# Matmuls of two PSUM banks interleaved, operand by operand, in the projections and the feed-forward layer of a one-core block

## The chip, the cores and the metric

The kernel runs on one core of one Trainium2 chip. The metric is the device time of one execution in microseconds. Five engines work side by side, each in the order of its own instructions: TensorE (matmuls; in the profile PE, and PEld for the loads of its stationary operand), VectorE (DVE), ScalarE (ACT), GpSimd (POOL) and SyncE (SP), whose queue issues the DMAs here. A matmul multiplies a stationary operand of 128 x 128, loaded by a LDWEIGHTS instruction, with a moving operand of 128 rows and up to 512 columns, and writes or accumulates into a bank of PSUM. There are eight banks of 512 fp32 columns.

## The reference, cut to what matters

One layer of a diffusion transformer on 1024 tokens of 1024 features, in fp32. The two products with large weights that the change touches most are `w_in` and the feed-forward pair:

```
px  = modulate(x, mx[0], mx[1]) @ w_in            # 1024 x 3840
mix = token_mixers(px, ...)                       # scans, short convolution, spatial gate
x1  = layer_norm(ALPHA * x + mx[2] * (mix @ w_out), ...)
h   = modulate(x1, mx[3], mx[4])
a, g = split(h @ ffn_up)                          # 1024 x 5632, two halves of 2816
a   = dwconv3x3(a as a 16 x 64 grid) + conv_b
ffn = (gelu(a) * g) @ ffn_down                    # 2816 -> 1024
out = layer_norm(ALPHA * x1 + mx[5] * ffn, ...)
```

Every fp32 product is computed as three float32r products. Both operands are split into a high part (rounded to float32r) and a low part (the exact rest), and high x high, high x low and low x high are accumulated in the same bank.

## The kernel before

`mm3` (L100 to L104) issues these three matmuls: L102 multiplies the high stationary part with the high moving part, L103 the same stationary part with the low moving part, L104 the low stationary part with the high moving part. All three go to one bank. L102, L103 and L104 therefore stand for nearly all matmuls in the profile.

A *unit* is 128 columns of a weight matrix against all 1024 tokens. It needs two banks, one for each half of the tokens, and 8 feature tiles (kt) x 3 matmuls for each half: 48 matmuls of 512 columns. Before, a unit runs through all 24 matmuls of the first half and then through the 24 of the second:

- `proj` and `proj_fm` compute a unit of `w_in`, in 20 places: three for each of the heads 1 to 3 (`z_head`), one for each head's gate (`gate_head`), five in `short_conv`, two in `spatial_gate`. Each is preceded by `load_unit`, which loads the weights in two DMAs and splits them on ScalarE (L82) and VectorE (L83).
- `banks_up` and `up_half` compute a unit of `ffn_up`. There are 44, taken in the order a(f), g(f), a(f+1), ... for f from 0 to 21. The first three units (0, 22, 1) are issued half by half in an order of their own, `self.first`.
- `ffn_down` works on a token half at a time with all eight banks: four token tiles (t) x two halves of the 1024 output columns (c). It runs over the 22 feature tiles f, and for each over t and c, with one `mm3` of 3 matmuls in each bank; here the stationary operand is a tile of the split activations (`hh`) and the weights move. The last 3 feature tiles of the first token half and the last 7 of the second are kept back as `late` and issued bank by bank at the end.

The banks come from two pools of four, A and B, each used in rotation (`bank`). All of `w_in`'s units use pool A. The scan stages (`scan_levels`, L575 and its neighbours) use B. In `ffn_up` the units of a use A and those of g use B. A bank is free again when its last reader is done. The readers are:

- in a scan head, ScalarE's sigmoids (`scan_z`);
- in `gate_head`, ScalarE (L663) and then VectorE (L664), after which L665 completes the head;
- in `spatial_gate`, VectorE (L824), which first needs the small matmuls of L820 and their evacuation L823;
- in `ffn_up`, for a the two ScalarE reads L953 and L954 of each half, after which VectorE runs the convolution (L964, eight instructions over the whole tile), ScalarE the GELU (L966) and VectorE the product with g (L970), which reads and so frees g's banks.

The order on each engine is made by the framework's planner. It takes instructions by priority (their order in the program, with weights and their splits pulled ahead by `AHEAD` = 350 places) as their inputs and tiles become available in its own timing model. On TensorE it so places scan matmuls between the matmuls of projections.

Of the kernel before, what the change touches and what calls it, by code (L numbers as in the profile page):

```python
# [16 lines left out]
P = 128  # L17
# [14 lines left out]
# columns of the packed per-partition parameters  # L32
# [9 lines left out]
def strided(t, off, dims):  # L42
    """An access pattern over the free bytes of an SBUF tile (offsets in elements)."""
    return bass.AP(t.tensor, t.offset + off, [list(t.ap[0])] + [list(d) for d in dims])


class Builder:
    AHEAD = 350        # how far weights run ahead of the program's order
# [10 lines left out]
    # ---------------------------------------------------------------- tiles  # L59
# [18 lines left out]
    # -------------------------------------------------------------- helpers  # L78
    def split(self, src, hi, lo):
        """hi = src rounded to float32r; lo = the exact rest of it."""  # L80
        nc = self.nc
        nc.scalar.copy(hi, src)  # L82
        nc.vector.tensor_tensor(out=lo, in0=src, in1=hi.bitcast(F32), op=ALU.subtract)  # L83

    def load_unit(self, src, shape, hl=None):
        """Weights from DRAM [128, 1024] into their high and low parts."""
        hi, lo = hl or (self.Wt(shape, nm="wh"), self.Wt(shape, nm="wl"))
        n = shape[0] // 2
        for i in range(2):
            c = slice(i * n, (i + 1) * n)  # L90
            self.load_split(src[:, c], hi[:, c], lo[:, c], (n, shape[1]))
        return hi, lo
# [12 lines left out]

    def rsqrt(self, y, v, n):
        """y = v ** -0.5 for a few columns: first guess from the bits, three Newton steps."""
        nc = self.nc
        t = self.small([n], nm="nwt", bufs=2)
        yi = y.bitcast(I32)  # L110
        nc.vector.tensor_scalar(out=yi, in0=v.bitcast(I32), scalar1=1, scalar2=None, op0=ALU.logical_shift_right)
        nc.vector.tensor_scalar(out=yi, in0=yi, scalar1=-1, scalar2=0x5F3759DF, op0=ALU.mult, op1=ALU.add)
        for _ in range(3):
            nc.vector.tensor_tensor(out=t, in0=v, in1=y, op=ALU.mult)
            nc.vector.scalar_tensor_tensor(out=t, in0=t, scalar=-0.5, in1=y, op0=ALU.mult, op1=ALU.mult)
            nc.vector.scalar_tensor_tensor(out=y, in0=t, scalar=1.5, in1=y, op0=ALU.add, op1=ALU.mult)

    def rsqrt2(self, y, v, n):
        """y = v ** -0.5: square root of ScalarE, reciprocal, one Newton step."""
        nc = self.nc  # L120
        t = self.small([n], nm="nwt1", bufs=4)
        nc.scalar.activation(t, v, AF.Sqrt)
        nc.vector.reciprocal(y, t)
        nc.vector.tensor_tensor(out=t, in0=v, in1=y, op=ALU.mult)
        nc.vector.scalar_tensor_tensor(out=t, in0=t, scalar=-0.5, in1=y, op0=ALU.mult, op1=ALU.mult)
        nc.vector.scalar_tensor_tensor(out=y, in0=t, scalar=1.5, in1=y, op0=ALU.add, op1=ALU.mult)

    def ln_stats(self, tiles, tag, act=False, st=None):
        """Mean and 1/sqrt(var + eps) over the free axis of each tile: [128, n, 2]."""
# [19 lines left out]
    def ln_stats_act(self, x, junk):  # L149
        """The same for one tile, the sums on ScalarE."""  # L150
# [15 lines left out]
    def ada_col(self, j, sc, dst, tiles):  # L166
        """One column of 128 modulations: ada_w[:, 128j:128j+128].T @ silu(c) + ada_b."""
# [14 lines left out]
    def after(self, t, j=5):  # L182
        """Holds a load into t back until the start-up has modulation j."""
        self.nc.vector.tensor_copy(t[:, 0:1], self.mods[:, j:j + 1])
# [11 lines left out]
    # ------------------------------------------------------------- the whole  # L196
    def build(self):
        tc, nc, a = self.tc, self.nc, self.a
        self.NR = 4
        with ExitStack() as ctx:  # L200
# [9 lines left out]
            # the scan's large tiles; later parts of w_out, then of h  # L210
# [30 lines left out]
    def alloc_x2(self, pool, g):  # L241
        """Modulated x_new, feature-major, for token half g: [k2][high, low] of [128, 2, 512]."""
# [15 lines left out]
    def consts2(self):  # L258
        nc = self.nc
        # lower bound: the running sum of a softmax over DEPTH = 1 rows, less its first row  # L260
# [14 lines left out]
        # masks[l][s, t] = 1 where s and t share a block of 2B but not one of B (B = 2**l)  # L275
# [6 lines left out]
        nc.vector.tensor_tensor(out=ii, in0=ii, in1=x, op=ALU.bitwise_xor)      # s xor t  # L282
# [4 lines left out]
    # --------------------------------------------------------------- start-up  # L287
    def startup(self):
        """x to feature-major xm (high, low); z_f, z_b, q of head 0, v of heads 0 and 1 and a part of the short convolution's
        gate as the features arrive, first for the first half of the tokens, then for the second."""  # L290
# [6 lines left out]
        # silu of c and of c_ctx, to come back as rows on every partition  # L297
# [15 lines left out]
        def norm(t, act, n=1):  # L313
            """LN of tiles t to t + n - 1; act: sums on ScalarE."""
# [67 lines left out]
        # products one step behind their features  # L382
# [34 lines left out]
    # ----------------------------------------------------------- token mixers  # L417
    def proj_fm(self, unit, banks):
        """128 columns of w_in for all tokens, features on the partitions."""
        hi, lo = unit  # L420
        for g in range(2):
            s = slice(g * 512, (g + 1) * 512)
            for kt in range(KT):
                self.mm3(banks[g], hi[:, kt, :], lo[:, kt, :], self.xh[kt][:, s], self.xl[kt][:, s], kt == 0, kt == KT - 1)
# [11 lines left out]
    def unit_tm(self, src, w=None):  # L436
        """256 columns, kt in two halves, for the token-major products."""
        return [self.load_unit(src[i], (4, 256), w and (w[:, 2 * i], w[:, 2 * i + 1])) for i in range(2)]

    def proj_tm(self, src, xh, xl, ntt, evac, w=None):  # L440
        """256 columns, tokens on the partitions; two token tiles in a bank."""
# [13 lines left out]
    def step(self, n):  # L455
        """The next pieces of the work that goes between other stages."""
        while n and self.aside:
            self.aside.pop(0)()
            n -= 1
# [60 lines left out]
    def scan_z(self, s, g, zf, zb, zq):  # L520
        """Sigmoids of z_f, z_b (and of their negatives) and silu(q) for token half g."""
# [9 lines left out]
    def scan_prep(self, s, h, z=None):  # L531
# [11 lines left out]
        # the factor 1 - lb of k goes with q, channel by channel  # L543
# [6 lines left out]
    def scan_levels(self, s):  # L550
        """Scores within chunks of 128: blocks of B against their neighbours, B doubling.

        kq holds (without 1 - lb, which q has) k_f * (decay from after s to its block's end), k_b * (decay from its
        block's start to before s), q * (decay from its block's start to t), q * (decay
        from t to its block's end); F[d] at B*j holds the decay over block j."""
# [9 lines left out]
        for l in range(7):  # L565
# [14 lines left out]
            # to blocks of 2B  # L580
# [12 lines left out]
    def scan_states(self, s, h, vt):  # L593
# [4 lines left out]
        for d in range(2):  # L598
# [3 lines left out]
            # the last chunk of a scan leaves no state  # L602
# [38 lines left out]
        # times 1 / sqrt(mean over the head's 128 values + eps), token by token  # L641
# [14 lines left out]
    def gate_head(self, O, h):  # L656
        """O * hg_norm_g * silu(g)"""
# [9 lines left out]
    def ctx_mods(self):  # L667
        """The context's normalised tiles and its modulations, in pieces."""
# [24 lines left out]
    def ctx_prep(self):  # L693
        """The context, modulated, feature-major, in high and low parts."""
# [14 lines left out]
    def ctx_states(self, ch, cl):  # L709
        """The states that the context leaves to both scans (without the factor 1 - lb)."""  # L710
# [6 lines left out]
        for h in range(H):  # L717
            fk = self.S((2, 2, TC), nm="cfk")     # [f_f, f_b], [k_f, k_b]
# [10 lines left out]
            for d in range(2):  # L729
# [4 lines left out]
                # decay from after s to the end (forward), from the start to before s (backward)  # L734
# [46 lines left out]
    def spatial_gate(self):  # L781
        nc, a = self.nc, self.a
        rows = self.S((2, 512), nm="sgrow")     # ln_g, ln_b
        nc.sync.dma_start(rows[:, 0, 0:256], a["sg_ln_g"].broadcast_to([P, 256]))
        nc.sync.dma_start(rows[:, 1, 0:256], a["sg_ln_b"].broadcast_to([P, 256]))
        wsb = self.S((6, P), nm="sgwb")         # w[g].T, then b_s over the two heads of each pair
# [41 lines left out]
    # -------------------------------------------------------- output projection  # L828
    def gate_row(self, m, row):
        """Modulation m as a row on every partition."""  # L830
# [13 lines left out]
    def ln_rows(self, y, lng, lnb):  # L844
        """y = LN(y) * lng + lnb, in place."""
# [5 lines left out]
    def wout_load(self, which, op=None):  # L851
        """w_out's rows with the gate (modulation 2) on their columns, in two parts."""
# [66 lines left out]
    def modulate2(self, pool, ys, t0):  # L919
        """LN and modulation 3, 4 of x_new's tiles from t0 on, feature-major into x2."""  # L920
# [18 lines left out]
    # ------------------------------------------------------------------- FFN  # L939
# [32 lines left out]
    def banks_up(self, f):  # L972
        """Columns f of ffn_up; the first few in an order that waits last for the second half of the tokens."""
# [10 lines left out]
        return [self.up_half(u, g, "A" if f < FT else "B") for g in range(2)]  # L984
# [8 lines left out]
    def ffn_down(self, dn):  # L993
        nc, a = self.nc, self.a
        rows = None
        for g in range(2):
# [8 lines left out]
            for f in range(FT):  # L1005
# [24 lines left out]
                if f < FT - LAST:  # L1030
                    for t in range(4):
                        for c in range(2):
                            work(t, c, f, hh, wh, wl)
# [39 lines left out]
    def finish(self, y, t, lng, lnb, st):  # L1073
        """out = LN(y) * lng + lnb"""
# [10 lines left out]
def layout(x):  # L1085
    """The inputs laid out for the kernel; values untouched."""
    import numpy as np
    c = np.ascontiguousarray
    w = x["w_in"][0]                                      # [1024, 3840]
    fm = w.reshape(KT, P, 30, P).transpose(2, 1, 0, 3)    # [30, 128 p, 8 kt, 128]  # L1090
    tm = lambda m: c(m.reshape(2, 4, P, -1, 256).transpose(3, 0, 2, 1, 4))   # [n, 2, 128 p, 4 kt, 256]
# [32 lines left out]
```

## Time and profile before

| | |
|---|---|
| runs of the kernel before | 1353.97 and 1355.95 us, median 1354.96 us |
| span of the profiled execution | 1354.2 us, 17543 instructions |
| stage of the mixers (projections, scans, gates) | to about 526 us |
| output projection and second modulation | about 526 to 634 us |
| ffn_up | about 634 to 1105.7 us |
| ffn_down | 1105.7 to about 1345 us, the final normalisation after it |
| DMA | 135.14 MB, 100 GB/s on average |

The page of the profile gives first the busy time of each engine, its share of the span and its instructions, then a strip of 40 slices in tenths, then the chain of work that ended last, and then groups of instructions by line. In such a group, `psA<-x,wh` is a matmul into a bank of pool A with a moving operand x and a stationary operand wh; `x352` is the count. The time that is printed for a matmul includes a modelled end that overlaps the next one, so the distance between the starts of two matmuls, or the length of a stretch over the count, is the pace.

### The profile page before, as it was taken

How to read it: one execution, taken by the hardware profiler on the slowest of the kernel's cores; microseconds unless marked ns; L12 is line 12 of the kernel's file. 1: busy time of each engine (PE TensorE's matmuls, PEld its weight loads, DVE VectorE, ACT ScalarE, POOL GpSimd, SP SyncE). 2: the span in 40 equal slices, each digit the busy share in tenths (PEclk: the TensorE clock that was granted, in tenths of full speed). 3: DMA queues.
4: the chain of work that ended last, by engine and by line, in shares of the span. 5: the costliest groups of instructions: out<-in, count | busy, mean ns of one | idle time of the engine just before them, and what ended most of it. 6: DMA issues, size and time to landing. Idle time of an engine off the chain costs nothing.

```text
span 1354.2 us, 17543 instructions
## 1 busy us (share of the span) xinstructions
PE 1319.4 (97%) x6730; PEld 1114.1 (82%) x6730; DVE 945.0 (70%) x1735; ACT 472.1 (35%) x878; POOL 1.7 (0%) x8
## 2 busy tenths in 40 slices
PE   4999999999999999999999999999999999999997
PEld 3888988898888887877888888888888888888885
DVE  7979954869688688886876757575656664349357
ACT  4744544433331424434322222222222233223330
POOL 0000000000000000000000000000000000000000
PEclk9999999999999999999999999999999999999998
DMA  9672410132131444221222111211111033235332
GB/s 331 249 242 77 133 63 31 32 116 81 40 112 60 137 148 156 99 104 62 95 77 78 63 63 47 68 50 54 47 47 47 31 115 135 93 109 201 111 105 82
DMA packets 60900, 135.14 MB, mean 100 GB/s; under 512 B 7168, under 2 KB 7824, under 8 KB 60816
## 3 DMA queue, kind: packets, MB, share of 16 engines
q1 hardware_dynamic: 60816, 134.02, 29.2%
q8 instruction: 53, 0.87, 0.3%
q14 instruction: 31, 0.25, 0.1%
HBM read 125.59 MB, written 8.40 MB: 99 GB/s over the span
## 4 chain that ended last, share of the span: by engine, by line
PE 82%; DVE 9%; DMA 4%; ACT 3%; issue 1%; DVEq 0%; SPq 0%; ACTq 0%
PE psA L102 16%; PE psA L103 16%; PE psA L104 16%; PE psB L103 9%; PE psB L102 9%; PE psB L104 9%; PE psB L575 4%; PE psB L614 1%; DMA r<-in_w_out 1%; DMA cada<-in_ada 1%; DVE adat L172 1%; ACT O L639 1%; DMA adat<-in_ada 1%; DVE bnst L137 1%; DVE wl L83 1%
## 5 line engine op out<-in xcount | busy, mean ns | idle before, releaser
L83 DVE TENSOR_TENSOR wl<-r,wh 128x512 fp32r<-128x512 f32 x160 | 104.3, 687 | 155.8 <-ACT wh L82 149.9
L82 ACT CAST wh<-r 128x512 fp32r<-128x512 f32 x160 | 92.5, 619 | 311.5 <-PE psB L103 160.7
L102 PE MATMUL psA<-x,wh 128*128 128x512 f32 x352 | 137.3, 390 | 0.8 <-ACT x L82 0.8
L104 PE MATMUL psA<-x,wl 128*128 128x512 f32 x352 | 137.2, 390 | 0.0
L103 PE MATMUL psA<-x,wh 128*128 128x512 f32 x352 | 137.2, 390 | 0.0
L102 PE MATMUL psB<-x,wh 128*128 128x512 f32 x352 | 137.0, 389 | 0.0
L104 PE MATMUL psB<-x,wl 128*128 128x512 f32 x352 | 136.9, 389 | 0.0
L103 PE MATMUL psB<-x,wh 128*128 128x512 f32 x352 | 136.9, 389 | 0.0
L102 PE MATMUL psA<-xh,wh 128*128 128x512 f32 x320 | 126.7, 396 | 0.0
L103 PE MATMUL psA<-xl,wh 128*128 128x512 f32 x320 | 126.4, 395 | 0.0
L104 PE MATMUL psA<-xh,wl 128*128 128x512 f32 x320 | 125.8, 393 | 0.0
L964 DVE SCALAR_TENSOR_TENSOR h<-a,par,h 128x945 f32<-128x945 f32 (+2 forms) x96 | 117.4, 1223 | 7.1 <-ACT a L954 4.2
L964 DVE SCALAR_TENSOR_TENSOR hk<-a,par,hk 128x945 f32<-128x945 f32 (+2 forms) x80 | 97.6, 1223 | 5.6 <-ACT a L954 3.4
L102 PEld LDWEIGHTS psA<-x,wh 128*128 128x128 f32 x352 | 66.0, 188 | 14.7 <-ACT x L82 1.2
L102 PEld LDWEIGHTS psB<-x,wh 128*128 128x128 f32 x352 | 66.1, 188 | 13.9 <-DVE x L83 0.3
L103 PEld LDWEIGHTS psB<-x,wh 128*128 128x128 f32 x352 | 66.1, 188 | 13.8
L103 PEld LDWEIGHTS psA<-x,wh 128*128 128x128 f32 x352 | 66.1, 188 | 13.6
L104 PEld LDWEIGHTS psB<-x,wl 128*128 128x128 f32 x352 | 66.1, 188 | 13.6
L104 PEld LDWEIGHTS psA<-x,wl 128*128 128x128 f32 x352 | 66.1, 188 | 13.6
L104 PEld LDWEIGHTS psA<-xh,wl 128*128 128x128 f32 x320 | 60.2, 188 | 11.8
L103 PEld LDWEIGHTS psA<-xl,wh 128*128 128x128 f32 x320 | 60.2, 188 | 11.8 <-issue 0.2
L102 PEld LDWEIGHTS psA<-xh,wh 128*128 128x128 f32 x320 | 60.2, 188 | 11.7 <-issue 0.2
(316 smaller groups left out, 2787.7 us busy)
## 6 DMA issues: line engine op xcount, KB each, us to landing
r<-in_wup SPq DMA_DIRECT2D x88, 256.0 KB, 2.7
r<-in_w_down SPq DMA_DIRECT2D x88, 256.0 KB, 2.9
r<-in_win SPq DMA_DIRECT2D x56, 256.0 KB, 2.8
ada<-in_ada SPq DMA_DIRECT2D x24, 512.0 KB, 3.8
adat<-in_ada SPq DMA_DIRECT2D x16, 512.0 KB, 6.7
r<-in_ada SPq DMA_DIRECT2D x26, 256.0 KB, 3.0
cada<-in_ada SPq DMA_DIRECT2D x11, 512.0 KB, 5.4
x<-in_x SPq DMA_DIRECT2D x8, 512.0 KB, 5.8
```

Of the source, the lines that this page charges most:

```text
L82: nc.scalar.copy(hi, src)
L83: nc.vector.tensor_tensor(out=lo, in0=src, in1=hi.bitcast(F32), op=ALU.subtract)
L102: mm(out, lh, rh, start=first, stop=False)
L103: mm(out, lh, rl, start=False, stop=False)
L104: mm(out, ll, rh, start=False, stop=last)
L137: nc.vector.bn_stats(out=st[:, c, :], in_=x[:, c * 512:(c + 1) * 512])
L172: nc.vector.tensor_tensor_reduce(out=t, in0=t, in1=sc[:, i * n:(i + 1) * n], scale=1.0, scalar=0.0 if i == 0 else acc[:, 0:1], op0=ALU.mul ...
L575: nc.tensor.matmul(b[:, c, :], A[:, t0:t0 + P], strided(kq, 3 * T + t0, [[2 * B, P // (2 * B)], [B - T, 2], [1, B]]), start=c == 0, stop=c ...
L614: nc.tensor.matmul(b[:, c, :], KTt[:, g * 4 + c, :], vt[:, g * 4 + c, hv], start=c == use[g][0], stop=c == use[g][-1])
L639: nc.scalar.activation(O[:, k, :], b[:, c, :], AF.Square, accum_out=ss[:, k:k + 1])
L964: nc.vector.scalar_tensor_tensor(out=o, in0=a3[:, r0 + di:r1 + di, c0 + dj:c1 + dj], scalar=cw(i, j), in1=o, op0=ALU.mult, op1=ALU.add)
```

## The change

A new helper `mm3_pair` takes two banks, one pair of stationary parts and two pairs of moving parts. It issues the six matmuls operand by operand, and each operand for both banks before the next. `proj_fm`, `banks_up` (all but the first three units) and the main part of `ffn_down` use it. In the units the loop over kt is now outermost, and both banks are allocated ahead of it. The `late` steps of `ffn_down`, `up_half` for the first three units, the token-major products (`proj_tm`), the start-up and the output projection keep `mm3`. Apart from this the diff removes comments and docstrings only.

```
+    def mm3_pair(self, outs, lh, ll, rhs, first, last):
+        mm = self.nc.tensor.matmul
+        for i, (l, r) in enumerate(((lh, 0), (lh, 1), (ll, 0))):
+            for o, m in zip(outs, rhs):
+                mm(o, l, m[r], start=first and i == 0, stop=last and i == 2)
...
     def proj_fm(self, unit, banks):
         hi, lo = unit
-        for g in range(2):
-            s = slice(g * 512, (g + 1) * 512)
-            for kt in range(KT):
-                self.mm3(banks[g], hi[:, kt, :], lo[:, kt, :], self.xh[kt][:, s], self.xl[kt][:, s], kt == 0, kt == KT - 1)
+        for kt in range(KT):
+            self.mm3_pair(banks, hi[:, kt, :], lo[:, kt, :],
+                          [(self.xh[kt][:, g * 512:(g + 1) * 512], self.xl[kt][:, g * 512:(g + 1) * 512]) for g in range(2)],
+                          kt == 0, kt == KT - 1)
...
         u = self.load_unit(self.a["wup"][f], (KT, P))
-        return [self.up_half(u, g, "A" if f < FT else "B") for g in range(2)]
+        banks = [self.bank("A" if f < FT else "B") for _ in range(2)]
+        for kt in range(KT):
+            x = [[self.x2[kt // 2][p][g][:, kt % 2, :] for p in range(2)] for g in range(2)]
+            self.mm3_pair(banks, u[0][:, kt, :], u[1][:, kt, :], x, kt == 0, kt == KT - 1)
+        return banks
...
                 if f < FT - LAST:
                     for t in range(4):
-                        for c in range(2):
-                            work(t, c, f, hh, wh, wl)
+                        s = slice(t * P, (t + 1) * P)
+                        self.mm3_pair(banks[t], hh[0][:, s], hh[1][:, s],
+                                      [(wh[:, c * 512:(c + 1) * 512], wl[:, c * 512:(c + 1) * 512]) for c in range(2)],
+                                      f == 0, f == FT - 1)
```

## The prediction

> **What bounds the kernel now.** I read the page's first two parts, then the chain, to see which engine is the limit and whether that holds in every stage.
>
> ```profile
> PE 1319.4 (97%) x6730; PEld 1114.1 (82%) x6730; DVE 945.0 (70%) x1735; ACT 472.1 (35%) x878; POOL 1.7 (0%) x8
> ...
> PE   4999999999999999999999999999999999999997
> ...
> PEclk9999999999999999999999999999999999999998
> ...
> PE 82%; DVE 9%; DMA 4%; ACT 3%; issue 1%; DVEq 0%; SPq 0%; ACTq 0%
> ```
>
> TensorE is full in every slice but the first and the last, at the full granted clock, and carries 82% of the chain. The time is therefore the number of matmuls times their pace, plus the moments in which TensorE waits. Those are few:
>
> ```profile
> PE psB L411 <- DVE x L163: 17.5, 3, 11.4
> PE psA L102 <- ACT xh L414: 1.3, 1, 1.3
> PE psA L103 <- DVE wl L83: 1.3, 1, 1.3
> PE psB L652 <- DVE OT L647: 1.1, 4, 0.3
> ...
> PE psA L103 <- DVE wo L83: 0.8, 1, 0.8
> PE psA L102 <- ACT x L82: 0.8, 1, 0.8
> ...
> PE psB L820 <- DVE vs L810: 0.4, 2, 0.2
> ```
>
> That is the view of waits for TensorE (total, times, longest). The 17.5 us are the start-up. All other waits sum to 7.8 us, so removing stalls can give little. What is left is the pace. The printed duration of a matmul overlaps its neighbours, so I take the pace from the table of stretches, as length over count:
>
> ```profile
> 470.20:488.20 18.00, 18.00 (x152) 18.00 (x151) 14.01 (x23) 7.63 (x13) 0.00 (x0) 1.00 0.43 134
> 700.00:1080.00 380.00, 380.00 (x1678) 314.53 (x1678) 242.69 (x265) 100.80 (x159) 0.00 (x0) 1.00 0.17 55
> 1115.00:1205.00 90.00, 90.00 (x398) 74.51 (x397) 34.64 (x55) 31.27 (x57) 0.00 (x0) 1.00 0.34 115
> ```
>
> The columns are length, then PE, PEld, DVE, ACT and POOL busy with counts, the granted clock, DMA. About two matmuls of a count only reach in over an edge. The first row is a stage of 256-column matmuls: 18.00 / 150 = 120.0 ns. The second is ffn_up, 512 columns, 24 in a row into one bank: 380 / 1676 = 226.7 ns. The third is ffn_down, where the bank changes every third matmul: 90 / 396 = 227.3 ns, or 226.7 with one more in the count. From 120.0 and 226.7, 256 columns stream in 106.7 ns and a fixed 13.3 ns comes with every matmul whatever its length. Those 13.3 ns are all that a better order could remove.
>
> **The change part by part.** First, how many matmuls it touches:
>
> ```profile
> L102 PE MATMUL psA<-x,wh 128*128 128x512 f32 x352 | 137.3, 390 | 0.8 <-ACT x L82 0.8
> L102 PE MATMUL psA<-xh,wh 128*128 128x512 f32 x320 | 126.7, 396 | 0.0
> L103 PEld LDWEIGHTS psB<-x,wh 128*128 128x128 f32 x352 | 66.1, 188 | 13.8
> L103 PEld LDWEIGHTS psA<-x,wh 128*128 128x128 f32 x352 | 66.1, 188 | 13.6
> ```
>
> Of ffn_up's 44 units 41 go the new way (the first three keep up_half): 41 x 48 = 1968. The projections' 320 per line are 320 x 3 = 960, that is 20 projections. ffn_down has 19 + 15 feature steps before its late ones, 24 matmuls each: 816. Together 3744 of 6730. None is added or removed, and no DMA, evacuation or load moves in the program.
>
> *Shared stationary operand.* Before, the second of each three (L103) has the same stationary operand as the first: 2 of 6 neighbours share. After, it is 4 of 6. The rows above say what sharing does now: L103 still has its own LDWEIGHTS, 352 for 352 matmuls, and the page counts 6730 loads for 6730 matmuls. The timeline around a change of bank shows its pace:
>
> ```profile
> 1094.16 0.39 PE L102 MATMUL psA<-x,wh 128*128 128x512 f32 x1
> 1094.39 0.39 PE L103 MATMUL psA<-x,wh 128*128 128x512 f32 x1
> 1094.62 0.39 PE L104 MATMUL psA<-x,wl 128*128 128x512 f32 x1
> 1094.84 0.39 PE L102 MATMUL psB<-x,wh 128*128 128x512 f32 x1
> 1095.07 0.39 PE L103 MATMUL psB<-x,wh 128*128 128x512 f32 x1
> ```
>
> L103 starts 0.23 us after L102 (same stationary operand), L104 0.23 after L103 (another one). Sharing is worth nothing here: cost 0.
>
> *No bank twice in a row.* L104 to L102 above goes to another bank and starts 0.22 us later, as within a bank, and the ffn_down stretch has the same 226.7 to 227.3 ns. Cost 0. What the trace never shows is both at once, another bank and the same stationary operand. I bound it by the nearest rows: at best the fixed 13.3 ns goes, at worst the pace is off by the 0.6 ns between the two stretches, 3744 x 0.6 = 2.2 us either way. I take 0, since each half alone shows 0; the best end is a rival below.
>
> [...]
>
> *Both banks finish together.* Before, a unit's first bank was complete 24 matmuls (5.4 us) ahead of its second, and was evacuated under it. Now both end with the unit, and both must be free at its start. In ffn_up the pools A and B alternate and a pair of banks comes back only three units (3 x 48 x 0.2267 = 32.6 us) after its end, so 5 us are covered. In the projections, all in pool A, a pair comes back after one unit, 10.9 us. The latest evacuation there is the first gated head's: its unit's last matmul starts at 385.69 us, its second bank is read at 393.59, and the unit that wants the bank starts at 400.72.
>
> ```profile
> 385.69 0.39 PE L104 MATMUL psA<-xh,wl 128*128 128x512 f32 x1
> ...
> 393.59 0.68 DVE L664 TENSOR_TENSOR G<-psA,G 128x512 f32<-128x512 f32 x1
> ...
> 400.72 0.39 PE L102 MATMUL psA<-xh,wh 128*128 128x512 f32 x1
> ```
>
> A second such read of 0.68 us ends at 394.95: 5.8 us to spare, cost 0. Two places are tighter.
>
> The last gated head takes the bank that the spatial gate reads last:
>
> ```profile
> 512.49 2.84 PE L820 MATMUL psB<-sgwb,vs 128*64 128x128 f32 x48 [0.22 <-DVE vs L810]
> 515.26 0.50 PE L103 MATMUL psA<-xl,wh 128*128 128x512 f32 x1
> 515.45 0.69 DVE L824 TENSOR_TENSOR sgo<-sgo,psA 128x512 f32<-128x512 f32 x1
> ...
> 534.73 0.50 PE L103 MATMUL psA<-wo,mh 128*128 128x512 f32 x1 [0.84 <-DVE wo L83]
> ```
>
> Its projection goes on at 515.26; a pair needs the second bank at once, and L824 frees it at 515.45 + 0.69 = 516.14. That is a new wait of up to 0.9 us. But TensorE waits 0.84 us at 534.73 anyway, for a part of w_out that arrives no later than now: the one wait goes into the other. I take 0; the ends are 0 and 0.9.
>
> At the turn from ffn_up to ffn_down the last convolution is late next:
>
> ```profile
> 1095.86 0.77 ACT L953 ACTIVATE h<-psA,par 128x512 f32<-128x512 f32 x1
> 1096.54 0.57 ACT L954 COPY a<-psA 128x512 f32<-128x512 f32 x1
> ...
> 1097.14 10.03 DVE L964 SCALAR_TENSOR_TENSOR h<-a,par,h 128x945 f32<-128x945 f32 x8 [0.38 <-ACT a L954]
> ...
> 1108.37 1.29 DVE L970 TENSOR_TENSOR h<-h,psB 128x512 f32<-128x512 f32 x2
> ...
> 1109.80 0.39 PE L102 MATMUL psB<-dwh,dhr 128*128 128x512 f32 x1
> 1110.03 0.39 PE L103 MATMUL psB<-dwl,dhr 128*128 128x512 f32 x1
> ```
>
> From ScalarE's first read of the second half (1095.86) to the convolution (1097.14) are 1.28 us. With both halves left to the end it is twice that, and L970, which frees the last two banks of pool B, ends at 1109.66 + 1.28 = 1110.94. ffn_down's fourth token tile takes these banks; as a pair its second matmul would start at 1110.03 and now waits to 1110.94: +0.9 us, with nothing behind it to absorb it. The ends are 0 (the planner puts other matmuls first) and 1.3.
>
> *The planner's order.* In the mixers it slots scan matmuls between projection matmuls. A new order can shift which of the small waits occur: by the wait rows at most all 7.8 us vanish or as much again appears. I take 0.
>
> **The sum.** The profiled execution spans 1354.2 us; 1354.2 + 0 + 0 + 0.9 = 1355.1. The runs' median, 1354.96, is 0.8 above that span, so 1355.9 us.
>
> **The rivals.**
> 1. *Faster: the fixed 13.3 ns goes where neighbours share the operand and change bank.* 3744 x 4/6 = 2496 matmuls x 13.3 ns = 33.2 us: 1355.9 - 33.2 = 1322.7. For it: only this combination is unseen, and two hidden causes of equal size would each alone show nothing. Against it: L103 pays in full for a repeated operand, a changed bank pays in full, and the load is issued every time. It decides at 27.1 / 2496 = 10.9 ns. Chance 5%.
> 2. *Slower: units wait for their pair of banks.* All 61 units (20 + 41) now ask for two free banks at their first matmul. A wait of 27.1 / 61 = 0.44 us at each is 2%; at 1 us each the time is 1355.9 + 61 = 1417. Against it: ffn_up has some 28 us to spare, the projections 5.8 us at the tightest ordinary place. Chance 3%.
> 3. *Slower: the clock drops.* At half clock the 213.4 ns of streaming double; 127 matmuls of it make 27.1 us, and the whole 3744 would give 1355.9 + 799 = 2155. The ffn_down stretch, which goes through eight banks in turn, has a granted clock of 1.00. Chance 1%. [...]
> 4. *The change does not do what it says*, because the planner breaks up the pairs: the time stays at 1355, inside my own case.
>
> **How the numbers follow.** My own case has 91%: 1355.9, with the pace's 2.2 us and about 7 us of shifted waits to either side, 1347 to 1365. Outside 2% (1327.9 to 1382.1, about what a measurement of this kernel can tell from no change) lie only rivals 1 to 3: faster 5%, slower 3 + 1 = 4%, the same 91%. The range 1347 to 1365 leaves out these 9% and some 8% for smaller gains or losses of pace.
>
> **What would show it.** The stretch inside ffn_up should again give 226 to 228 ns per matmul with as many loads as matmuls; 215 there would prove rival 1. The granted clock stays 1.00. A TensorE wait of about 0.9 us for L970 should appear at the start of ffn_down, and the wait at 534.73 should shrink if one appears at 515. Conversely a TensorE wait on ScalarE or VectorE readers of pool A or B at many units would prove rival 2. I am wrong above all if repeated operand and changed bank together differ from either alone.

## The result and the profile after

| | before | after |
|---|---|---|
| median of the runs | 1354.96 us | 1367.74 us (1367.71 and 1367.77) |
| span of the profiled execution | 1354.2 us | 1365.9 us |
| mean granted clock of TensorE | 0.997 | 0.995 |

The ratio is 1.0092, with a 95% interval of 1.0062 to 1.0121: 12.8 us slower, within 2%, and above the predicted range of 1347 to 1365. In the changed kernel all matmuls of pairs stand on L111, and the lines of before that lie behind the new helper are 7 higher (L663 is L670, L664 is L671, L665 is L672, L970 is L977).

The page of the changed kernel: busy time and the strip of 40 slices for TensorE.

```profile
PE 1322.1 (97%) x6730; PEld 1113.8 (82%) x6730; DVE 941.7 (69%) x1735; ACT 469.4 (34%) x878; POOL 1.7 (0%) x8
...
PE   4999999999999997999999999999999999999997
```

The work is the same, with a load for each matmul as before. The strip has one new digit: a 7 in slice 16, 512 to 546 us, where the output projection begins. The stretch inside ffn_up, in the view of stretches (length, then PE, PEld, DVE, ACT and POOL busy, the granted clock, DMA):

```profile
700.00:1080.00 380.00, 380.00 (x1678) 314.53 (x1677) 243.41 (x271) 98.52 (x157) 0.00 (x0) 1.00 0.18 57
```

1678 matmuls in 380 us again: the pace has not moved. What moved are waits. The view of waits of TensorE (total, times, longest):

```profile
PE psA L104 <- DVE ml L83: 3.7, 1, 3.7
PE psA L102 <- ACT mh L82: 3.2, 1, 3.2
PE psA L111 <- ACT wh L82: 1.5, 1, 1.5
PE psA L103 <- DVE xl L422: 1.3, 1, 1.3
...
PE psB L111 <- DVE h L977: 1.1, 1, 1.1
```

The first two and the last are new. mh and ml are the split parts of the mixers' output, one token tile at a time: the operand with which `out_proj` begins. The timeline of TensorE there (start, length, then the instruction, and in brackets the idle time before it and its releaser):

```profile
528.87 0.61 PE L111 MATMUL psA<-xh,wl 128*128 128x512 f32 x2
532.69 0.50 PE L102 MATMUL psA<-wok,mh 128*128 128x512 f32 x1 [3.21 <-ACT mh L82]
...
533.49 0.40 PE L103 MATMUL psA<-wok,mh 128*128 128x512 f32 x1
537.54 0.80 PE L104 MATMUL psA<-wok,ml 128*128 128x512 f32 x1 [3.66 <-DVE ml L83]
538.13 0.63 PE L102 MATMUL psA<-wok,mh 128*128 128x512 f32 x1
538.56 0.63 PE L103 MATMUL psA<-wok,mh 128*128 128x512 f32 x1
...
541.00 0.39 PE L103 MATMUL psA<-wok,mh 128*128 128x512 f32 x1
```

At 528.87 the last two matmuls of the last gated head's unit start. In the 8.7 us from there to 537.54 TensorE starts only four more, and the ones behind the second wait start 0.43 us apart instead of 0.23. From 537.54 to 541.00 are 8 steps: 3.46 us where 8 x 0.23 = 1.84 are usual, 1.6 more; the granted clock there is 0.55 on average. The two waits and the slow steps make 3.2 + 3.7 + 1.6 = 8.5 us; the 0.84 us at 534.73 that before had is gone, so 7.7 net. With the 1.1 us on h that is 8.8 of the 11.7 by which the spans differ. (The row names h because L977, which frees the bank as it reads g out of it, writes h.)

Why is mh late? ScalarE's timeline, first before, then after:

```profile
520.80 0.60 ACT L663 ACTIVATE G<-psA 128x512 f32<-128x512 f32 x1 [25.35 <-PE psA L104]
521.30 0.49 ACT L82 CAST mh<-O 128x128 fp32r<-128x128 f32 x2
```

```profile
529.29 0.60 ACT L670 ACTIVATE G<-psA 128x512 f32<-128x512 f32 x1 [31.15 <-PE psA L111]
529.79 2.16 ACT L82 CAST wo<-r 128x512 fp32r<-128x512 f32 x4
531.86 0.60 ACT L670 ACTIVATE G<-psA 128x512 f32<-128x512 f32 x1
532.35 0.49 ACT L82 CAST mh<-O 128x128 fp32r<-128x128 f32 x2
```

In both kernels ScalarE stands idle for 25 to 31 us in front of its first read of the last head's banks, and the splits mh come behind that read. Before, the first bank was complete in the middle of the unit, so the read, and with it the splits, ran under the second half. Now the first bank is complete only when the unit ends. VectorE repeats the pattern for ml:

```profile
529.92 0.69 DVE L671 TENSOR_TENSOR G<-psA,G 128x512 f32<-128x512 f32 x1 [5.35 <-ACT G L670]
530.53 2.49 DVE L83 TENSOR_TENSOR wo<-r,wo 128x512 fp32r<-128x512 f32 x4
532.93 0.68 DVE L671 TENSOR_TENSOR G<-psA,G 128x512 f32<-128x512 f32 x1
...
534.68 1.28 DVE L672 SCALAR_TENSOR_TENSOR O<-O,par,G 128x1024 f32<-128x1024 f32 x1
535.88 1.29 DVE L881 TENSOR_TENSOR r<-r,gate 128x512 f32<-128x512 f32 x2
...
537.20 0.28 DVE L83 TENSOR_TENSOR ml<-O,mh 128x128 fp32r<-128x128 f32 x1
```

ml is at the end of a row of 7.3 us of VectorE work that began when the unit ended, and none of that work is ml's own input. (Its inputs are mh, split at 532.35, and the output O of an earlier head; L672 writes the O of the last head.)

### The profile page after: what moved, and what is told of

Read it like the earlier page. It is cut to its first block, busy times and chain, and to the rows that moved or that the text cites. A ratio compares the mean times of both kernels' runs of the same rounds, so it can differ in the third digit from the quotient of the medians.

```text
span 1365.9 us, 17541 instructions
## 1 busy us (share of the span) xinstructions
PE 1322.1 (97%) x6730; PEld 1113.8 (82%) x6730; DVE 941.7 (69%) x1735; ACT 469.4 (34%) x878; POOL 1.7 (0%) x8
## 4 chain that ended last, share of the span: by engine, by line
PE 81%; DVE 10%; ACT 4%; DMA 3%; issue 2%; DVEq 0%; SPq 0%; ACTq 0%
PE psA L111 35%; PE psB L111 23%; PE psA L104 4%; PE psA L102 4%; PE psA L103 4%; PE psB L582 4%; DMA cada<-in_ada 1%; PE psB L621 1%; DVE adat L179 1%; PE psB L102 1%; PE psB L104 1%; PE psB L103 1%; ACT O L646 1%; DVE h L971 1%; DVE wl L83 1%
## 5 line engine op out<-in xcount | busy, mean ns | idle before, releaser
L83 DVE TENSOR_TENSOR wl<-r,wh 128x512 fp32r<-128x512 f32 x160 | 104.0, 687 | 126.2 <-ACT wh L82 126.2
L111 PE MATMUL psB<-x,wh 128*128 128x512 f32 x672 | 179.6, 389 | 0.0
L111 PE MATMUL psA<-x,wh 128*128 128x512 f32 x640 | 171.1, 389 | 0.0
L111 PEld LDWEIGHTS psB<-x,wh 128*128 128x128 f32 x672 | 126.1, 188 | 26.2
L111 PEld LDWEIGHTS psA<-x,wh 128*128 128x128 f32 x640 | 120.0, 188 | 25.1
L111 PE MATMUL psB<-x,wl 128*128 128x512 f32 x336 | 103.4, 389 | 0.0
L111 PE MATMUL psA<-xh,wh 128*128 128x512 f32 x320 | 101.1, 394 | 1.6 <-ACT wh L82 1.5
L111 PE MATMUL psA<-xh,wl 128*128 128x512 f32 x320 | 102.2, 396 | 0.0
L111 PE MATMUL psA<-xl,wh 128*128 128x512 f32 x320 | 101.5, 394 | 0.0
L111 PE MATMUL psA<-x,wl 128*128 128x512 f32 x320 | 98.4, 389 | 0.0
L111 PE MATMUL psB<-dwh,dh 128*128 128x512 f32 x264 | 76.1, 389 | 0.0
L111 PE MATMUL psA<-dwh,dh 128*128 128x512 f32 x264 | 76.0, 389 | 0.0
L111 PEld LDWEIGHTS psB<-x,wl 128*128 128x128 f32 x336 | 63.1, 188 | 13.1
L111 PEld LDWEIGHTS psA<-xh,wh 128*128 128x128 f32 x320 | 59.2, 188 | 13.9 <-ACT wh L82 1.9
L111 PEld LDWEIGHTS psA<-x,wl 128*128 128x128 f32 x320 | 60.1, 188 | 12.5
L111 PEld LDWEIGHTS psA<-xl,wh 128*128 128x128 f32 x320 | 59.7, 188 | 12.2 <-issue 0.2
L111 PEld LDWEIGHTS psA<-xh,wl 128*128 128x128 f32 x320 | 59.2, 188 | 11.5 <-issue 0.2
L582 PE MATMUL psB<-kq,A 128*128 128x128 f32 x448 | 60.1, 288 | 0.9 <-ACT A L576 0.7
L582 PEld LDWEIGHTS psB<-kq,A 128*128 128x128 f32 x448 | 55.7, 192 | 6.1 <-ACT A L576 5.7
```

The lines of the kernel that those rows point to most:

```text
L111: mm(o, l, m[r], start=first and i == 0, stop=last and i == 2)
L582: nc.tensor.matmul(b[:, c, :], A[:, t0:t0 + P], strided(kq, 3 * T + t0, [[2 * B, P // (2 * B)], [B - T, 2], [1, B]]), start=c == 0, stop=c ...
```

## The experiments

Three theories. *Theory 1*: in-order queues. The splits of the output projection's first token tile stand behind the last head's reads on ScalarE and VectorE, and a pair lets those reads begin only at the unit's end; one unit of 61 carries nearly all of the loss. *Theory 2*: the loss is spread over the mixers, where both banks of each unit end together. *Theory 3*: the pairs themselves run slower. One expectation below names a fourth as rival 4 (not that of the prediction): both banks come free too late for the next writer. Kernels were timed against the kernel before on the same chip. Its medians there were 1355.32 us (for gate3_by_bank, before_late_bank_first, ffn_pairs_only and proj_pairs_only), 1354.48 us (for before_gate3_pair, split0_before_reads, gate3_down0_by_bank and after_fill) and 1355.43 us (for split0_last_a_by_bank and before_split0_first). Its single executions lay between 1352.55 and 1359.16 us.

### One unit bank after bank

**gate3_by_bank**: the changed kernel, only the last gated head's unit as before.

```
-        z = self.proj(16 + h)
+        z = self.proj(16 + h, pair=h < H - 1)    # pair=False: the loop of before in proj_fm
```

> The changed kernel, but the unit of the last gated head (one of 61 pair units) runs bank after bank as before. Theory 1, queue: the time is lost where the output projection starts, because its operands' splits stand in ScalarE's and VectorE's queues behind the last head's reads, and with a pair both reads come only when the unit ends; TensorE's two waits there are 3.2 and 3.7 us against 0.8 before. Then 5 to 7 us come back: 1361 to 1363 us, and both waits go. Theory 2, spread: pairs upset the order of the whole mixer stage and the last head only shows the sum: 1366 to 1368 us, the waits move elsewhere. Theory 3, pace of pairs: 1367 us.

Measured: 1357.7 us, ratio 1.0016 [1.0006, 1.0025]. Both waits are gone from its list of waits, whose longest behind the start-up is now 1.5 us, and with them the slow steps; h stays:

```profile
PE psB L111 <- DVE h L982: 1.2, 1, 1.2
```

This speaks for theory 1 and against 2 and 3. It gave back about 10 us where 5 to 7 were expected, which the slow steps below explain in part.

### The converse: one unit as a pair

**before_gate3_pair**: the kernel before, with `mm3_pair` in that unit alone (`z = self.proj(16 + h, pair=h == H - 1)`).

> The kernel before with one part of the change alone: only the unit of the last gated head has its two banks interleaved. Theory 1: nearly all of the loss, 8 to 10 us, so 1363 to 1366, with the waits on mh and ml there. Theory 2: one unit of 61, 1355 to 1356.

Measured: 1364.16 us, ratio 1.0072 [1.0058, 1.0085]. Its two longest waits behind the start-up are the same as in the changed kernel:

```profile
PE psA L104 <- DVE ml L83: 3.7, 1, 3.7
PE psA L102 <- ACT mh L82: 3.2, 1, 3.2
```

So 48 of the 3744 matmuls that changed order cost 0.7% of the time.

### No pair at all, the late bank read first

**before_late_bank_first**: the kernel before, all banks filled as there; only the order of the last head's two reads is turned in the program.

```
-        for g in range(2):
+        for g in range(2) if h < H - 1 else (1, 0):
```

> The kernel before, without any pair; only the last gated head evacuates its two banks in the order second, first in the program. The planner then puts the splits of the output projection behind both of the head's reads on ScalarE, as in the changed kernel. Theory 1, queue: TensorE waits for mh and ml at the start of the output projection, though every unit still runs bank after bank: 3 to 6 us above before, 1358 to 1361 us. Theories 2 and 3: within 1 us of before, 1354 to 1356 us.

Measured: 1360.7 us, ratio 1.004 [1.0026, 1.0054]. Both waits appear though every unit runs bank after bank:

```profile
PE psA L104 <- DVE ml L83: 2.9, 1, 2.9
...
PE psA L102 <- ACT mh L82: 0.9, 1, 0.9
```

ScalarE's timeline shows what the edit did:

```profile
524.42 0.60 ACT L663 ACTIVATE G<-psA 128x512 f32<-128x512 f32 x1 [25.21 <-PE psA L104]
...
529.86 0.60 ACT L663 ACTIVATE G<-psA 128x512 f32<-128x512 f32 x1 [2.48 <-PE psA L104]
530.35 0.49 ACT L82 CAST mh<-O 128x128 fp32r<-128x128 f32 x2
```

The bank that is complete first is still read first, in the middle of the unit. But the splits mh now stand behind the second read, which comes only when the unit ends (its last matmul starts at 529.43). That fits theory 1 alone. (The profiled execution, 1364.1 us of span, lies above the median; its list also has a wait of 2.6 us on wl at 469 us, in the mixers, which is not part of this effect.)

### The halves of the change

**ffn_pairs_only** keeps the pairs of `ffn_up` and `ffn_down` and computes all projections bank after bank; **proj_pairs_only** is the reverse.

```
-    def proj_fm(self, unit, banks):
+    def proj_fm(self, unit, banks, pair=False):          # ffn_pairs_only
...
+        return [self.up_half(u, g, "A" if f < FT else "B") for g in range(2)]   # proj_pairs_only, and work(t, c, ...) in ffn_down
```

> Pairs in ffn_up and ffn_down only (2784 of the 3744 matmuls); all projections bank after bank. Theories 1 and 2: only the wait for L977 at the start of ffn_down is left, 1.3 us: 1356 to 1357 us. Theory 3, pace: 2784/3744 of the 12.8 us, 9.5 us: 1364 us.

> Pairs in the 20 projections only (960 of the 3744 matmuls); ffn_up and ffn_down as before. Theories 1 and 2: all but the 1.3 us of ffn_down: 1366 to 1367 us. Theory 3, pace: 960/3744 of the 12.8 us, 3.3 us: 1358 us.

Measured: 1357.08 us, ratio 1.0012 [1.0003, 1.0021], and 1365.01 us, ratio 1.007 [1.0058, 1.0082]. The projections alone came out 1 us under what was expected; their wait on ml is 2.8 us instead of 3.7. The 2784 paired matmuls of the feed-forward layer cost at most 0.2%. The list of waits of ffn_pairs_only has the one on h, and one on xl in the start-up, where nothing is paired:

```profile
PE psA L103 <- DVE xl L422: 1.2, 1, 1.2
PE psB L111 <- DVE h L982: 1.1, 1, 1.1
```

Theory 3 falls.

### The suspected queue, with every pair kept

**split0_before_reads**: the changed kernel with all its pairs; the first token tile's seven splits that do not need the last head are issued between that head's matmuls and its reads. The eighth stays where it was.

```
         z = self.proj(16 + h)
+        if h == H - 1:
+            self.early_split()       # split() of mix[kt][:, 0:P] for kt in self.order[:-1]
         G = self.S(nm="G")
...
-        split(0)
+        mh, ml = mhl[0] = self.early
+        self.split(self.mix[order[-1]][:, 0:P], mh[:, order[-1], :], ml[:, order[-1], :])
```

> All pairs stay as in the changed kernel, the unit of the last gated head included. Only the order of work on ScalarE and VectorE differs: the first token tile's seven splits that do not need the last head stand ahead of the last head's reads. Theory 1 (the splits wait behind reads that come late): the two waits on mh and ml, 3.2 and 3.7 us, go, and so does the slow stretch behind them, so the time falls by 7 to 9 us to 1359 to 1361. Theory 2 (the loss is in the unit itself or spread over the mixers): 1366 to 1368. Rival 4 (both banks are free too late for the next writer): the waits stay, 1366 to 1368.

Measured: 1356.99 us, ratio 1.0017 [1.0008, 1.0026], better than expected. ScalarE's timeline, with L672 for the read, and TensorE's:

```profile
519.48 0.30 ACT L82 CAST mh<-sgo 128x128 fp32r<-128x128 f32 x1 [1.29 <-DVE sgo L838]
527.62 0.60 ACT L672 ACTIVATE G<-psA 128x512 f32<-128x512 f32 x1 [7.84 <-PE psA L111]
```

```profile
527.20 0.62 PE L111 MATMUL psA<-xh,wl 128*128 128x512 f32 x2
527.66 0.40 PE L102 MATMUL psA<-wok,mh 128*128 128x512 f32 x1
...
528.13 0.39 PE L104 MATMUL psA<-wok,ml 128*128 128x512 f32 x1
```

The last of the seven splits starts as soon as its input, the spatial gate's sgo, is there, and is done 8 us ahead of the first read. So in the changed kernel it was their place in the queue, and no input, that held the splits back. (Why the planner had put them behind the reads is not shown.) TensorE goes from the unit into the output projection without a gap. Theory 1 is shown by adding the suspected cost where no pair is, and by taking it away where all pairs are.

### The rest of the loss

The wait on h at the start of `ffn_down` is what is left. **gate3_down0_by_bank**: gate3_by_bank, and the first step of `ffn_down` bank after bank too (`if g == 0 and f == 0: work(t, c, ...)`).

> The changed kernel with the unit of the last gated head bank after bank, as in gate3_by_bank, and the first step of ffn_down too (f = 0, g = 0). Theory 1: the wait on h of 1.2 us goes as well, and what is left of the pairs costs nothing: 1355 to 1357, 1 to 1.5 below gate3_by_bank. If the remaining 2 us were the price of the pairs themselves: no change, 1357 to 1358.

Measured: 1359.11 us, ratio 1.0034 [1.0023, 1.0046]: a miss. The order in which `ffn_down` asks for its banks does not matter, for the wait is as long as it was:

```profile
PE psB L102 <- DVE h L982: 1.1, 1, 1.1
```

Why it is 1.4 us above gate3_by_bank stays open; its wait on xl of 1.6 us at 92 us, in the start-up, was 0.2 in gate3_by_bank, and neither edit touches that stage.

The cause of the wait lies in the unit before the last, the last convolved one. ScalarE's timeline of the changed kernel behind that unit, then VectorE's:

```profile
1105.81 0.77 ACT L960 ACTIVATE h<-psA,par 128x512 f32<-128x512 f32 x1
...
1106.95 0.79 ACT L960 ACTIVATE h<-psA,par 128x512 f32<-128x512 f32 x1
```

```profile
1108.25 8.79 DVE L971 SCALAR_TENSOR_TENSOR h<-a,par,h 128x945 f32<-128x945 f32 x7 [1.53 <-ACT a L961]
1116.95 1.29 DVE L83 TENSOR_TENSOR dwl<-r,dwh 128x512 fp32r<-128x512 f32 x2
1118.16 1.20 DVE L971 SCALAR_TENSOR_TENSOR h<-a,par,h 128x945 f32<-128x945 f32 x1
1120.54 0.69 DVE L977 TENSOR_TENSOR h<-h,psB 128x512 f32<-128x512 f32 x1 [1.18 <-ACT h L973]
```

L960 and the copy L961 of each half, shown by the two L960, all come behind the unit. So the convolution begins 3.2 us after the unit ends (at 1105.01, when the next one starts) instead of 2.3 (1094.84 to 1097.14 before), 0.9 us later. A second delay comes on top: two weight splits (L83) now stand ahead of the eighth convolution instruction, where before they stood behind all eight, and GELU and the product wait 1.2 us more. Together the first product ends some 2 us later, at 1121.23, and the matmul that waits for it, at 1121.28, is the first one of a pair. So the order within the pair does not matter. **split0_last_a_by_bank**: split0_before_reads, and that one unit bank after bank.

```
+        if f == FT - 1:
+            return [self.up_half(u, g, "A") for g in range(2)]
```

> split0_before_reads, and beside it the last convolved unit of ffn_up (f = FT - 1) bank after bank. By the trace the wait on h at the start of ffn_down comes from a unit earlier than it looks: with a pair both banks of that unit end together, ScalarE reads the first of them (0.67 and 0.50 us) only then, and the convolution and all behind it start some 1.2 us later. If so, the wait of 1.1 us on h is gone and the time is 1 to 1.5 us under split0_before_reads (1356.99 there, so 1355.5 to 1356), the time of before. If the wait comes from the following unit (the gate's), it stays and the time does not change.

Measured: 1355.61 us, ratio 1.0004 [0.9995, 1.0013]. The reads (L968 there) are apart again, the first half's under the second half. The eight convolution instructions follow one another without the two splits between them, and no wait on h is left in its list of waits:

```profile
1090.70 0.78 ACT L968 ACTIVATE h<-psA,par 128x512 f32<-128x512 f32 x1 [0.50 <-PE psA L104]
...
1096.95 0.77 ACT L968 ACTIVATE h<-psA,par 128x512 f32<-128x512 f32 x1
```

With 60 of 61 units still paired, nothing measurable is left of the loss, and nothing is gained either.

**before_split0_first**: the kernel before with the early splits, no pair.

> The kernel before with the seven early splits of the first token tile ahead of the last head's reads, and no pair. There they are ready in time already, so by theory 1 nothing is to be gained but part of the 0.8 us wait on wo at 534.73: 0 to 1 us under before. A gain of more would mean that the order of the two queues costs the kernel before as well.

Measured: 1355.35 us, ratio 0.9999 [0.999, 1.0008]. In the kernel before the queue costs nothing that these runs can measure. No version tried here beats it.

### The slow steps

**after_fill**: the changed kernel with 26 further matmuls, in the two waits. The program issues them as 12 and 14; as the planner orders them, 15 fall into the first wait and 11 into the second.

```
+    for _ in range(12 if kt == order[0] else 14):     # t == c == 0, the first two kt
+        nc.tensor.matmul(warm, wh[order[0]][:, 0:P], wh[order[0]][:, 512:1024], start=True, stop=True)
```

> The changed kernel with 26 further matmuls of 128x512 whose results nothing reads, 15 in the wait on mh and 11 in the wait on ml, so that TensorE is busy while it would wait. The 26 add no time if they fit into the waits (15 x 0.227 = 3.4 us beside 3.2, 11 x 0.227 = 2.5 beside 3.7). If the slow matmuls behind the second wait (427 ns from start to start at a granted clock of 0.50) come from the idleness, they run at 227 to 235 ns and the clock stays at 1.00 there: 1365.5 to 1367. If they come from something else (transfers, operands), they stay slow: 1367 to 1369.

Measured: 1365.69 us, ratio 1.0079 [1.0063, 1.0094]. The interval overlaps that of the changed kernel, so the timeline of TensorE decides:

```profile
527.47 3.56 PE L911 MATMUL psB<-wok 128*128 128x512 f32 x15
...
531.41 2.70 PE L911 MATMUL psB<-wok 128*128 128x512 f32 x11
...
535.69 0.51 PE L104 MATMUL psA<-wok,ml 128*128 128x512 f32 x1 [1.11 <-DVE ml L83]
536.03 0.39 PE L102 MATMUL psA<-wok,mh 128*128 128x512 f32 x1
536.26 0.39 PE L103 MATMUL psA<-wok,mh 128*128 128x512 f32 x1
```

ml is as late as before (8.2 us behind the start of the filling), but from 536.03 on the steps behind it take 0.23 us, and the granted clock is 1.00 from 530 to 546 us. The slow steps came from TensorE's own idleness, not from transfers or operands.

## Why the prediction was wrong

- **Pace: right.** 226.7 ns, as many loads as matmuls; neither the shared operand nor the changed bank is worth anything, alone or together. Rival 1 falls.
- **Both banks finish together, ordinary units: right.** No reader of pool A or B shows up as a wait at many units; rival 2 is not what happened.
- **The last gated head: wrong, and this is the step that failed.** The prediction asked when the unit's own banks come free ("a new wait of up to 0.9 us", "I take 0; the ends are 0 and 0.9"). It did not ask what stands behind the readers of the unit's result. On ScalarE and VectorE these readers hold the head of the queue until the unit ends (ScalarE stands idle for 31.15 us ahead of its read), with the output projection's first operands behind them. In place of 0 to 0.9 the runs showed 7.7 us in the trace and 9.7 us in the median when this unit alone is paired. The row that would have told it was in the trace of before: 520.80, with 25.35 us of idle time ahead of the read and the splits right behind.
- **"The one wait goes into the other": half right.** The 0.84 us at 534.73 did vanish, but into two waits that together are eight times as long. The new wait at 515 did not appear: TensorE's longest there is 0.3 us, on vs.
- **The turn to ffn_down: the place and the releaser right, the size in part by luck.** 0.9 us was predicted, with L970 as the releaser and the doubled reads as the cause. A 1.1 us wait on it was measured, and it went when that one unit was undone. But the reads brought 0.9 us of delay and not 1.28, the two weight splits ahead of the last convolution instruction brought another 1.2, and the wait fell on the first matmul of the pair, not on its second.
- **The planner's order: undecided.** In the mixers a 1.5 us wait on wh came and the 1.3 us on wl went; the xl wait of 1.3 us does not come from pairs, for it is 1.2 in ffn_pairs_only, where no projection is paired, and 1.0 in before_split0_first, which has no pair at all. About 2.9 of the 11.7 us between the two spans are left to small differences of this kind, which is less than single executions of the kernel before differ by (1352.55 to 1359.16 us). In the medians split0_last_a_by_bank, with 60 of 61 units paired, bounds what is left to between -0.05 and 0.13%.
- **Rival 3, the clock: wrong cause, and small.** The clock did fall, to 0.50, which cost 1.6 us, but after a wait and not through the changes of bank: in the stretch inside ffn_up, where the bank now changes with every matmul, it is 1.00.

## What to carry to other kernels

When a change makes two results finish together instead of one after the other, follow the first result's reader in its engine's queue and list what stands behind it: that work loses its cover too, even if it has nothing to do with the result. Look hardest at the last unit of a stage, where the next stage's first operands are prepared. And cost a stall of TensorE above its own length: here waits of 3.2 and 3.7 us brought 1.6 us more, in the slow steps behind them.

## What the runs showed of the hardware

The granted clock of TensorE fell to 0.50 at waits of 2.9 to 3.2 us, and its matmuls of 512 columns then started 0.43 us apart in place of 0.23. The view of stretches of the changed kernel (after the counts, the granted clock):

```profile
530.00:534.00 4.00, 1.19 (x4) 0.67 (x4) 4.00 (x7) 3.83 (x12) 0.00 (x0) 0.98 0.51 160
...
534.00:538.00 4.00, 0.46 (x1) 0.46 (x2) 4.00 (x8) 1.70 (x5) 0.00 (x0) 0.50 0.80 245
```

The four matmuls behind the first wait, 3.21 us, still ran at full pace: the clock is 1.00 from 533.0 to 533.7 us, and the last three start 0.23 and 0.24 us apart. A mean of 0.98 over 4 us is 0.16 us at 0.50, so the clock fell at about 533.8. That is some 0.3 us after the last of the four had started (533.49) and before the second wait had lasted 0.2 us: the first wait brought it down, about 1.1 us after its end. In proj_pairs_only the clock fell within the first wait, which was as long (3.21 us): 0.87 over 3 us puts the fall at about 530.2.

```profile
528.00:531.00 3.00, 0.19 (x1) 0.00 (x0) 2.37 (x4) 3.00 (x6) 0.00 (x0) 0.87 0.34 125
```

In before_late_bank_first, where a wait of 0.9 us had ended at 530.70, it fell within the wait of 2.9 us on ml, which ended at 535.81: 0.63 over 534 to 538 us puts the fall at about 535.0. The wait of 1.5 us on wh in the changed kernel left it at 1.00 (456 to 460 us). So the length of a wait does not settle by itself when the clock falls; what else does, these runs do not show.
